# Row sums of reciprocals: loads of eight rows, the halves of every row added on TensorE, one product in four made on VectorE from a half copied to PSUM

## The chip, the cores and the metric

The kernel runs on one core of one Trainium2 chip. The metric is the device time of one execution in microseconds (us). Executions are compared with executions of the kernel before in the same rounds on the same chip.

## The reference

```python
def setup_inputs():
    batch, seq, dim = 32, 512, 1024
    return {"x": np.abs(np.random.randn(batch, seq, dim)).astype(np.float32) + 1e-6}

def reference(x):
    return np.sum(1.0 / x, axis=-1).astype(np.float32)
```

There are 16384 rows of 1024 float32, 128 rows in each of 128 partitions: 67.11 MB to read, 64 KB to write.

## The kernel before

Each row is split into two halves a and b of 512. As 1/a + 1/b = (a + b) / (ab), one reciprocal serves two elements: a product of the halves, then exp(-ln(ab)) on ScalarE, then a multiply by a + b with a running sum on VectorE. The sum a + b comes either from TensorE, as two matmuls with an identity that add up in PSUM (kind B), or is never formed: VectorE then multiplies the whole row of 1024 by the reciprocal, broadcast to both halves (kind A). Kind C gives one row whole to ScalarE.

```python
A, B, C = (2, 0, GP, False), (2, 0, GP, True), (1, 1, GP, False)
GROUPS = ([A, B, A, B, C, B, A, B] * 7 + ...)          # two rows in a group
xpool = ... bufs=16        # rpool, spool: 2 PSUM buffers each
for np_, ns, eng, on_pe in GROUPS:
    xt = xpool.tile([P, n, D], f32, tag="xt")
    nc.sync.dma_start(out=xt, in_=x_v[:, c0 : c0 + n, :])            # 1 MiB
    eng.tensor_tensor(out=pr, in0=xt[:, :np_, :H], in1=xt[:, :np_, H:], op=mult)
    if on_pe:
        for j in range(np_):
            for h in range(2):
                nc.tensor.matmul(sm[:, j, :], lhsT=ident,
                                 rhs=xt[:, j, h * H : (h + 1) * H],
                                 start=h == 0, stop=h == 1)
    ...                                                  # kind C's row on ScalarE
    nc.scalar.activation(out=pr, in_=pr, func=Ln, scale=S)
    nc.scalar.activation(out=rc, in_=pr, func=Exp, scale=-1.0)
    for j in range(np_):                  # rows of A: 1024 wide, of B: 512 wide
        nc.vector.tensor_tensor_reduce(out=row, in0=row, in1=rec, ..., accum_out=...)
```

## Time and profile before

| | before |
|---|---|
| time, median of the runs at hand before the change | 175.4 us |
| span of the profiled run | 172.6 us |
| rate of the loads in the middle (20 to 150 us) | 421 GB/s |
| rows that TensorE adds | 64 of 128 |
| TensorE busy, share of the span | 70% |

The prediction below shows the busy shares, the rates and the chain. Three groups of the same page give the durations that the argument uses; the columns are line, engine, operation, output and inputs, shapes, count, then busy us, mean ns of one, and idle time before them with what ended most of it.

```profile
L85 POOL TENSOR_TENSOR pr<-xt 128x1024 f32<-128x1024 f32 (+1 forms) x66 | 142.7, 2166 | 21.1 <-DMA xt<-in_x_dram 15.2
L90 PE MATMUL sm<-xt,ident 128*128 128x512 f32 x256 | 120.9, 617 | 47.0 <-DMA xt<-in_x_dram 45.0
L118 DVE CUSTOM_DVE_ANT_1 xt<-xt,rc 128x1024 f32<-128x1024 f32 x57 | 67.7, 1219 | 50.2 <-issue 27.2
```

GpSimd (POOL) has the least idle time, and TensorE's idle time is ended by landing loads: engines that wait for data. Each float32 matmul has two records in the trace. The mean of 617 ns is the length of one record; records overlap, and in a full stretch the next one starts 0.43 us later.

### The profile page before, as it was taken

How to read it: one execution, taken by the hardware profiler on the slowest of the kernel's cores; microseconds unless marked ns; L12 is line 12 of the kernel's file. 1: busy time of each engine (PE TensorE's matmuls, PEld its weight loads, DVE VectorE, ACT ScalarE, POOL GpSimd, SP SyncE). 2: the span in 40 equal slices, each digit the busy share in tenths (PEclk: the TensorE clock that was granted, in tenths of full speed). 3: DMA queues.
4: the chain of work that ended last, by engine and by line, in shares of the span. 5: the costliest groups of instructions: out<-in, count | busy, mean ns of one | idle time of the engine just before them, and what ended most of it. 6: DMA issues, size and time to landing. Idle time of an engine off the chain costs nothing.

```text
span 172.6 us, 1342 instructions
## 1 busy us (share of the span) xinstructions
PE 120.9 (70%) x256; PEld 47.4 (27%) x256; DVE 109.8 (64%) x243; ACT 142.0 (82%) x156; POOL 143.4 (83%) x72
## 2 busy tenths in 40 slices
PE   0099776767876767788666668977667876669480
PEld 0043322222332222233322223422222332223130
DVE  0009757874776757775578847468576755787791
ACT  2159989899878998889888996889988898988981
POOL 1599699969989799987999688997999979999920
PEclk9999999999999999999999996999999999999999
DMA  5999999999999999999999999999999999999500
GB/s 190 416 433 425 423 420 423 421 421 423 418 425 420 423 418 423 423 420 423 421 421 420 423 414 423 421 420 420 425 418 425 425 420 421 421 412 408 220 0 15
DMA packets 9799, 67.25 MB, mean 390 GB/s; under 512 B 1088, under 2 KB 1216, under 8 KB 1984
## 3 DMA queue, kind: packets, MB, share of 16 engines
q1 hardware_dynamic: 9792, 67.18, 94.0%
q8 instruction: 2, 0.03, 0.1%
q14 instruction: 5, 0.04, 0.1%
HBM read 67.11 MB, written 0.07 MB: 389 GB/s over the span
## 4 chain that ended last, share of the span: by engine, by line
DMA 78%; POOL 11%; ACT 2%; issue 2%; DVE 2%; SPq 1%; PE 1%; POOLq 0%; DVEq 0%
DMA xt<-in_x_dram 78%; POOL pr L85 11%; SPq L83 1%; ACT pr L106 1%; PE sm L90 1%; DVE xt L118 1%; ACT rc L111 1%; DVE pr L118 0%; ACT pr L111 0%; DVE pr L85 0%; POOLq L85 0%; DVE sums L118 0%; DVEq L118 0%; DVEq L157 0%
## 5 line engine op out<-in xcount | busy, mean ns | idle before, releaser
L85 POOL TENSOR_TENSOR pr<-xt 128x1024 f32<-128x1024 f32 (+1 forms) x66 | 142.7, 2166 | 21.1 <-DMA xt<-in_x_dram 15.2
L90 PE MATMUL sm<-xt,ident 128*128 128x512 f32 x256 | 120.9, 617 | 47.0 <-DMA xt<-in_x_dram 45.0
L118 DVE CUSTOM_DVE_ANT_1 xt<-xt,rc 128x1024 f32<-128x1024 f32 x57 | 67.7, 1219 | 50.2 <-issue 27.2
L106 ACT ACTIVATE pr<-pr 128x1024 f32<-128x1024 f32 (+1 forms) x67 | 65.0, 970 | 24.5 <-POOL pr L85 23.7
L90 PEld LDWEIGHTS sm<-xt,ident 128*128 128x128 f32 x256 | 47.4, 195 | 119.7 <-issue 57.8
L118 DVE CUSTOM_DVE_ANT_0 pr<-pr,sm 128x512 f32<-128x512 f32 x64 | 41.6, 685 | 9.8 <-ACT pr L111 8.6
L111 ACT ACTIVATE pr<-pr 128x1024 f32<-128x1024 f32 (+1 forms) x34 | 34.2, 1006 | 1.0
L111 ACT ACTIVATE rc<-pr 128x1024 f32<-128x1024 f32 (+1 forms) x33 | 29.9, 906 | 0.8
L118 DVE DVE_READ_ACCUMULATOR2_ANT sums<- 128x1 f32 x121 | 10.0, 82 | 0.0
L99 ACT ACTIVATE xt<-xt 128x1024 f32<-128x1024 f32 x7 | 7.3, 1041 | 0.0
L98 ACT ACTIVATE xt<-xt 128x1024 f32<-128x1024 f32 x7 | 7.3, 1040 | 0.0
L55 ACT ACT_TABLE_LOAD x1 | 1.3, 1283 | 0.7 <-PEq L146 0.7
L99 ACT ACTIVATION_READ_ACCUMULATOR xt<-xt 128x1 f32 x7 | 1.3, 186 | 0.0
L85 DVE TENSOR_TENSOR pr<-xt 128x512 f32<-128x512 f32 x1 | 0.7, 689 | 0.0
masks.py:197 POOL MEMSET ident<- 128x128 f32 x1 | 0.2, 204 | 0.3 <-POOLq L146 0.3
masks.py:199 POOL TENSOR_SCALAR_AFFINE_SELECT ident<-ident 128x128 f32<-128x128 f32 x1 | 0.3, 292 | 0.1
L146 POOL MEMSET const-float32-0.0<- 128x1 f32 x1 | 0.1, 98 | 0.2 <-issue 0.2
L146 POOL MEMSET const-bfloat16-1.0<- 128x1 bf16 x1 | 0.1, 101 | 0.0
L146 POOL MEMSET const-uint8-127<- 128x1 uint8 x1 | 0.1, 101 | 0.0
L146 POOL MEMSET const-float32-1.0<- 128x1 f32 x1 | 0.1, 98 | 0.0
## 6 DMA issues: line engine op xcount, KB each, us to landing
xt<-in_x_dram SPq DMA_DIRECT2D x61, 1024.0 KB, 19.8
xt<-in_x_dram SPq DMA_DIRECT2D x6, 512.0 KB, 15.6
out_dram<-sums SPq DMA_DIRECT2D x1, 64.0 KB, 1.5
```

Of the source, the lines that this page charges most:

```text
L55: nc.scalar.add_instruction(mybir.InstLoadActFuncSet(name=nc.get_next_instruction_name(), act_func_set_id=act_sets.index("natural_log_exp_ ...
L83: nc.sync.dma_start(out=xt, in_=x_v[:, c0 : c0 + n, :])
L85: eng.tensor_tensor(out=pr, in0=xt[:, :np_, :H], in1=xt[:, :np_, H:], op=mult)
L90: nc.tensor.matmul(sm[:, j, :], lhsT=ident, rhs=xt[:, j, h * H : (h + 1) * H], start=h == 0, stop=h == 1,)
L98: nc.scalar.activation(out=xt[:, j, :], in_=xt[:, j, :], func=Ln)
L99: nc.scalar.activation(out=xt[:, j, :], in_=xt[:, j, :], func=Exp, scale=-1.0, accum_out=sums[:, c0 + j : c0 + j + 1],)
L106: nc.scalar.activation(out=pr, in_=pr, func=Ln, scale=S)
L111: nc.scalar.activation(out=rc, in_=pr, func=Exp, scale=-1.0)
L118: nc.vector.tensor_tensor_reduce(out=row, in0=row, in1=rec, scale=S, scalar=0.0, op0=mult, op1=add, accum_out=sums[:, c0 + j : c0 + j + 1],)
L146: nc = _bacc.Bacc("TRN2", target_bir_lowering=False, num_devices=1)
```

## The change

The intent: larger transfers, which shrink row by row at the end so that little work is left after the last byte; a relief of VectorE from rows 1024 wide and of GpSimd from one product in four. VectorE makes that product from one half in SBUF and one in PSUM, to which TensorE copies it. A load holds one or two chunks. A chunk is the rows that are worked as one piece: one product on GpSimd for most of its rows, one Ln and one Exp on ScalarE for all of them.

```diff
+    LOADS = (
+        [[(4, 1), (4, 1)]] * 12
+        + [[(4, 1), (3, 1)], [(3, 1), (3, 1)], [(3, 1), (2, 1)], [(4, 1)]]
+        + [[(3, 1)], [(2, 0)], [(2, 1)], [(1, 0)], [(1, 1)], [(1, 1)]]
+    )
+    DIRECT = 126
-    xpool = ctx.enter_context(tc.tile_pool(name="xpool", bufs=16))
+    xpool = ctx.enter_context(tc.tile_pool(name="xpool", bufs=4))
...          spool: 6 PSUM banks for sums, bpool: 2 for copies
+        for m, v in chunks:                       # m rows, v products on VectorE
+            g = m - v
+            if g:
+                nc.gpsimd.tensor_tensor(
+                    out=pr[:, :g, :], in0=xc[:, :g, :H], in1=xc[:, :g, H:], op=mult
+                )
+            for j in range(g, m):
+                if c0 + q + j >= DIRECT:
+                    b = xc[:, j, H:]
+                else:
+                    b = bpool.tile([P, H], f32, tag="b")
+                    nc.tensor.matmul(b, lhsT=ident, rhs=xc[:, j, H:])
+                i = nc.vector.tensor_tensor(
+                    out=pr[:, j, :], in0=xc[:, j, :H], in1=b, op=mult
+                )
+                keep(i)                           # VectorE's order is fixed
+            if waiting:
+                sum_rows(*waiting)                # sums of the chunk before
+            for j in range(m):
+                s = spool.tile([P, H], f32, tag="s")
+                for h in range(2):
+                    nc.tensor.matmul(s, lhsT=ident, ...)
...          Ln, Exp on the whole chunk
```

More of the change, by code (lines that the diff above doesn't have):

```diff
@@ L33 @@
     S = float(2**17)
-    GP, DV = nc.gpsimd, nc.vector
-    A, B, C = (2, 0, GP, False), (2, 0, GP, True), (1, 1, GP, False)
-    GROUPS = (
-        [A, B, A, B, C, B, A, B] * 7
-        + [A, B, A, B, A]
-        + [(1, 0, GP, True), (1, 0, GP, False)] * 2
-        + [(1, 0, GP, True), (1, 0, DV, True)]
+    LOADS = (
+        [[(4, 1), (4, 1)]] * 12
+        + [[(4, 1), (3, 1)], [(3, 1), (3, 1)], [(3, 1), (2, 1)], [(4, 1)]]
+        + [[(3, 1)], [(2, 0)], [(2, 1)], [(1, 0)], [(1, 1)], [(1, 1)]]
     )
+    DIRECT = 126
     Ln = mybir.ActivationFunctionType.Ln
@@ L62 @@
     )
-    xpool = ctx.enter_context(tc.tile_pool(name="xpool", bufs=16))
+    xpool = ctx.enter_context(tc.tile_pool(name="xpool", bufs=4))
+    epool = ctx.enter_context(tc.tile_pool(name="epool", bufs=1))
     ppool = ctx.enter_context(tc.tile_pool(name="ppool", bufs=4))
     opool = ctx.enter_context(tc.tile_pool(name="opool", bufs=1))
-    rpool = ctx.enter_context(
-        tc.tile_pool(name="rpool", bufs=2, space=bass.MemoryType.PSUM)
-    )
-    spool = ctx.enter_context(
-        tc.tile_pool(name="spool", bufs=2, space=bass.MemoryType.PSUM)
+    spool = ctx.enter_context(
+        tc.tile_pool(name="spool", bufs=6, space=bass.MemoryType.PSUM)
+    )
+    bpool = ctx.enter_context(
+        tc.tile_pool(name="bpool", bufs=2, space=bass.MemoryType.PSUM)
     )
@@ L77, with sum_rows @@
     make_identity(nc, ident)
-    c0 = 0
-    for np_, ns, eng, on_pe in GROUPS:
-        n = np_ + ns
-        xt = xpool.tile([P, n, D], f32, tag="xt")
-        nc.sync.dma_start(out=xt, in_=x_v[:, c0 : c0 + n, :])
-        pr = ppool.tile([P, np_, H], f32, tag="pr")
-        eng.tensor_tensor(out=pr, in0=xt[:, :np_, :H], in1=xt[:, :np_, H:], op=mult)
-        if on_pe:
-            sm = spool.tile([P, np_, H], f32, tag="sm")
-            for j in range(np_):
-                for h in range(2):
-                    nc.tensor.matmul(
-                        sm[:, j, :],
-                        lhsT=ident,
-                        rhs=xt[:, j, h * H : (h + 1) * H],
-                        start=h == 0,
-                        stop=h == 1,
-                    )
-        for j in range(np_, n):
-            nc.scalar.activation(out=xt[:, j, :], in_=xt[:, j, :], func=Ln)
-            nc.scalar.activation(
-                out=xt[:, j, :],
-                in_=xt[:, j, :],
-                func=Exp,
-                scale=-1.0,
-                accum_out=sums[:, c0 + j : c0 + j + 1],
-            )
-        nc.scalar.activation(out=pr, in_=pr, func=Ln, scale=S)
-        if on_pe:
-            rc = pr
-        else:
-            rc = rpool.tile([P, np_, H], f32, tag="rc")
-        nc.scalar.activation(out=rc, in_=pr, func=Exp, scale=-1.0)
-        for j in range(np_):
-            if on_pe:
-                row, rec = rc[:, j, :], sm[:, j, :]
-            else:
-                row = xt[:, j, :].rearrange("p (h e) -> p h e", h=2)
-                rec = rc[:, j, :].unsqueeze(1).to_broadcast([P, 2, H])
-            nc.vector.tensor_tensor_reduce(
-                out=row,
-                in0=row,
-                in1=rec,
+    keep = tc.keep_in_program_order
+    def sum_rows(c, rc, sm):
+        for j, s in enumerate(sm):
+            i = nc.vector.tensor_tensor_reduce(
+                out=rc[:, j, :],
+                in0=rc[:, j, :],
+                in1=s,
                 scale=S,
@@ L125 @@
                 op1=add,
-                accum_out=sums[:, c0 + j : c0 + j + 1],
+                accum_out=sums[:, c + j : c + j + 1],
             )
+            keep(i)
+    waiting = None
+    c0 = 0
+    for k, chunks in enumerate(LOADS):
+        n = sum(m for m, _ in chunks)
+        if n > 3:
+            xt = xpool.tile([P, n, D], f32, tag="xt")
+        else:
+            xt = epool.tile([P, n, D], f32, tag=f"x{k}")
+        i = nc.sync.dma_start(out=xt, in_=x_v[:, c0 : c0 + n, :])
+        keep(i)
+        q = 0
+        for m, v in chunks:
+            xc = xt[:, q : q + m, :]
+            pr = ppool.tile([P, m, H], f32, tag="pr")
+            g = m - v
[6 more added lines that the diff above has]
+                    b = xc[:, j, H:]
+                else:
+                    b = bpool.tile([P, H], f32, tag="b")
[3 more added lines that the diff above has]
+                )
+                keep(i)
+            if waiting:
+                sum_rows(*waiting)
+            sm = []
+            for j in range(m):
+                s = spool.tile([P, H], f32, tag="s")
+                for h in range(2):
+                    nc.tensor.matmul(
+                        s,
+                        lhsT=ident,
+                        rhs=xc[:, j, h * H : (h + 1) * H],
+                        start=h == 0,
+                        stop=h == 1,
+                    )
+                sm.append(s)
+            nc.scalar.activation(out=pr, in_=pr, func=Ln, scale=S)
+            nc.scalar.activation(out=pr, in_=pr, func=Exp, scale=-1.0)
+            waiting = c0 + q, pr, sm
+            q += m
         c0 += n
     assert c0 == F, c0
+    sum_rows(*waiting)
     nc.sync.dma_start(out=out_v, in_=sums)
```

## The prediction

> **What bounds the kernel now.** I read the page first (busy shares, the slices, the chain of work that ended last), then the timeline of single engines, because busy shares alone do not say what an engine could do if it were kept full.
>
> From the page of the kernel before: busy time by engine, the granted clock and the rate of the transfers by slice, and the chain.
>
> ```profile
> span 172.6 us, 1342 instructions
> PE 120.9 (70%) x256; PEld 47.4 (27%) x256; DVE 109.8 (64%) x243; ACT 142.0 (82%) x156; POOL 143.4 (83%) x72
> ...
> PEclk9999999999999999999999996999999999999999
> ...
> GB/s 190 416 433 425 423 420 423 421 421 423 418 425 420 423 418 423 423 420 423 421 421 420 423 414 423 421 420 420 425 418 425 425 420 421 421 412 408 220 0 15
> ...
> DMA 78%; POOL 11%; ACT 2%; issue 2%; DVE 2%; SPq 1%; PE 1%; POOLq 0%; DVEq 0%
> ```
>
> The reader is to see a flat rate near 421 GB/s from the second slice almost to the end, and a chain that is 78% transfers. The input is 128 rows per partition, 67.11 MB; 67.11 / 421 = 159.4 us. About 3 us lie before the stream runs and about 10 after it, which gives the span of 172.6. So the input stream is the bound, and the only gain open to any change is in those two ends. Each four rows arrive in 4 x 0.524 = 2.1 MB / 421 GB/s = 4.98 us; every engine has to do four rows in less than that.
>
> Now what TensorE needs. The timeline of PE in the middle, and of the weight loads (PEld) in one of those bursts and at the start:
>
> ```profile
> 63.63 3.67 PE L90 MATMUL sm<-xt,ident 128*128 128x512 f32 x8 [1.36 <-DMA xt<-in_x_dram]
> 68.55 3.67 PE L90 MATMUL sm<-xt,ident 128*128 128x512 f32 x8 [1.24 <-DMA xt<-in_x_dram]
> 73.52 3.67 PE L90 MATMUL sm<-xt,ident 128*128 128x512 f32 x8 [1.30 <-DMA xt<-in_x_dram]
> ```
>
> ```profile
> 9.52 0.34 PEld L90 LDWEIGHTS sm<-xt,ident 128*128 128x128 f32 x1 [0.52 <-issue]
> 10.37 0.34 PEld L90 LDWEIGHTS sm<-xt,ident 128*128 128x128 f32 x1 [0.52 <-issue]
> ...
> 14.40 0.19 PEld L90 LDWEIGHTS sm<-xt,ident 128*128 128x128 f32 x1 [0.24 <-issue]
> 14.83 0.19 PEld L90 LDWEIGHTS sm<-xt,ident 128*128 128x128 f32 x1 [0.24 <-issue]
> 15.26 0.19 PEld L90 LDWEIGHTS sm<-xt,ident 128*128 128x128 f32 x1 [0.24 <-issue]
> 15.69 0.19 PEld L90 LDWEIGHTS sm<-xt,ident 128*128 128x128 f32 x1 [0.24 <-issue]
> 16.12 0.19 PEld L90 LDWEIGHTS sm<-xt,ident 128*128 128x128 f32 x1 [0.24 <-issue]
> 16.55 0.19 PEld L90 LDWEIGHTS sm<-xt,ident 128*128 128x128 f32 x1 [0.24 <-issue]
> ```
>
> The program has 128 matmuls (64 rows on TensorE, two halves each), the trace has 256: each float32 matmul runs as two records, each with its own weight load. In a full stretch the loads start 0.43 us apart ((16.55 - 14.40) / 5), so one float32 matmul of 512 columns costs 0.86 us, and one row (two halves) 1.72 us. A burst of 8 records is two rows: 8 x 0.43 = 3.44, plus the drain of the last, 3.67. One such burst comes per four rows arriving (4.97 us), and PE then waits 1.3 us for the next load. TensorE looks 70% busy with only half of the rows. That is the number that decides this case. At 9.5 to 12.1 the same loads stand 0.85 apart: the cold clock.
>
> The end, from the timeline of all engines: the last sum on VectorE, and the start of the store.
>
> ```profile
> 169.09 0.69 DVE L118 CUSTOM_DVE_ANT_0 pr<-pr,sm 128x512 f32<-128x512 f32 x1 [0.75 <-ACT pr L111]
> 169.70 0.08 DVE L118 DVE_READ_ACCUMULATOR2_ANT sums<- 128x1 f32 x1
> 169.81 0.35 SPq L131 DMA_DIRECT2D out_dram<-sums  x1
> ```
>
> From the end of the last sum (169.78) to the end of the span are 2.8 us.
>
> **What the Trainium skill says.** "TensorE: Matmul & The Clock Gate", section "Back-to-back issue gap", gives N / 2.4 + 2.5 ns for a warm stream: 216 ns for 512 columns of one pass. "FP8 and Floating Point Precision", section "TensorE Precision Notes", says that true FP32 takes four passes through the array: 4 x 216 = 863 ns. The trace agrees: 2 x 0.43 = 0.86 us. The first page's Part 1 on the clock gate says that the array starts at half clock for some 3.4 us of activity; the trace shows 0.85 against 0.43 us for about 4 us, and once more near 105 us after an idle stretch of 3 us. "DMA: Bandwidth & Descriptors", "Rules for kernel authors", asks for at least 1 MiB per transfer, and its Specifications give a fabric ceiling of 435 GB/s. The loads before are already 1 MiB, and 421 is 97% of that ceiling, so loads of eight rows have almost nothing left to win.
>
> **The change part by part.**
>
> Removed: the VectorE sums over 1024 columns with a broadcast reciprocal (57 of 1219 ns) and the seven rows that ScalarE did whole. Every row now goes by the halves: product of the halves, Ln, Exp of 512 columns, times the sum of the halves from TensorE.
>
> GpSimd: three rows of four. From 2365 ns for 1024 columns and 1273 for 512, 1536 columns cost 2365 + 1092 = 3.46 us per four rows, against 4.98 of arrival. It falls from 83% and stops being near the bound.
>
> ScalarE: 1055 ns for 1024 and 615 for 512 give about 1.94 us for 2048 columns, so Ln and Exp cost 3.9 us per four rows. Below 4.98.
>
> VectorE: one product at 0.69 and four sums, which start 0.61 apart in the trace before: 3.1 us per four rows.
>
> TensorE: four rows x two halves, plus one copied half = 9 float32 matmuls = 9 x 0.86 = 7.74 us per four rows. That is above 4.98, by 55%. TensorE becomes the bound, and the stream of loads waits for it through the four buffers of eight rows.
>
> Total: 128 x 2 = 256 matmuls for the sums. Of the 35 rows whose product VectorE makes, the last two are read directly, so 33 copies; the built program's order shows 33 too. 289 x 0.86 = 248.5 us of TensorE, in one unbroken run if nothing starves it.
>
> Start: PE needs the first load of eight rows. In the kernel before the first eight rows are loads 1 to 4: the first product starts at 5.58, the second load is there at 8.5, then 2.5 us each, so the fourth lands near 13.5. The order of bytes is the same, so PE starts near 13.5 instead of 8.5. The cold clock costs once about 2.3 us (five spacings of 0.85 instead of 0.43, and a partial one). The last matmul drains in 0.3, its sum takes 0.8 on VectorE (ScalarE's part of that row is ready, since the last loads landed long before), the store 2.8.
>
> Sum: 13.5 + 2.3 + 248.5 + 0.3 + 0.8 + 2.8 = 268.2 us of span. The measured run of the profile before was 174.8 for a span of 172.6, 2.2 more: 270.4, and I say 270.5 us.
>
> **The rivals.**
>
> First: the stream stays the bound, and the shorter tail wins some us (170 to 174). For it speaks that PE's busy share counts overlapping records and drains, so 70% overstates the need. Against it: the weight-load spacing is not a busy share, and within the bursts PE waited for no data. For this rival a float32 matmul would have to cost under 4.98 / 9 = 0.55 us, and the trace has none below 0.86.
>
> Second: a PSUM wait makes it worse than the TensorE sum. There are six banks for sums, four used per chunk, so the third row of a chunk waits for the first sum of the chunk before. Reckoned from the start of a chunk on PE: the copy is there at 0.9, the product at 1.7, Ln and Exp done at 5.7; VectorE, kept in order, first does the next chunk's product, possible at 7.74 + 0.9, so that the first sum ends near 10.2; PE asks for that bank at 7.74 + 0.86 + 2 x 1.72 = 12.0. About 1.8 us to spare, so no wait. If ScalarE or a semaphore took 2 us more than I reckon, a stall of 0.5 us in each of some 30 chunks would add 15 us: 285.
>
> Third: the clock. A TensorE that runs full could be granted less. Before, it was 0.99 on average with one dip to 0.6 after an idle stretch; a full engine has fewer such stretches, which speaks for none. A loss of 3% would add 8 us: 278.
>
> Fourth: the reverse, PE starts earlier or packs better than 0.43: at most the 5 us of the later start, 265.
>
> **Range and chances.** The central sum has one large term, measured in a stretch that is like the whole of the new kernel, and four small ones known to about 1 us each. The rivals add on the upper side, the fourth takes off a little: 264 to 278. For a time below 179 TensorE would have to do 9 matmuls in about 5.2 us per chunk; I see no way to it. Faster 0.01, same 0.01, slower 0.98.
>
> **What would show it.** PE has 578 records, loads of weights 0.43 us apart throughout, and the chain of what ended last is mostly PE instead of DMA. GB/s falls from 421 to about 2.1 MB / 7.74 us = 271 in the middle slices, after the first buffers are full; the queue's waits are for PE or its followers. PE's first matmul starts near 13.5 and the last one near 264. GpSimd, ScalarE and VectorE each fall to about half busy. Wrong would be: weight loads less than 0.4 apart; regular gaps in PE of over 0.3 us released by VectorE (the second rival); a granted clock below 0.97 in the middle slices (the third); GB/s still at 420 (the first).

## The result, and the profile after

Measured: 268.87 us (median of 4, 268.59 to 269.28) against 175.06 us before. The ratio is 1.536 (95% interval 1.531 to 1.542). Ratios here are the mean time of one kernel's fast runs over that of the other's of the same rounds, so not quite the ratio of the medians quoted.

The page of the changed kernel, as the prediction showed it of before:

```profile
span 267.5 us, 1796 instructions
PE 250.7 (94%) x578; PEld 110.7 (41%) x578; DVE 102.1 (38%) x291; ACT 125.6 (47%) x75; POOL 108.1 (40%) x41
...
PEclk9999999999999999999999999999999999999999
...
GB/s 289 431 436 431 431 431 446 417 439 201 432 88 392 157 353 277 225 402 78 441 108 382 245 246 308 107 364 20 374 0 265 423 404 9 0 0 0 1 0 10
...
PE 93%; DMA 5%; DVE 0%; ACT 0%; issue 0%; DVEq 0%
PE s L128 82%; PE b L117 11%; DMA xt<-in_x_dram 5%; DVE pr L81 0%; ACT pr L137 0%; ACT pr L136 0%; DVE pr L118 0%; DVEq L170 0%
...
L128 PE MATMUL s<-xt,ident 128*128 128x512 f32 x512 | 226.6, 595 | 0.0
```

TensorE is busy from its first matmul to its last: 250.7 us of 267.5, with no idle time at all before the sums. The chain, which was 78% transfers, is 93% TensorE: 82% sums, 11% copies. After the first slice the loads run near 431 GB/s for eight slices, until the four buffers are full, and then in bursts. The other three engines have fallen to 38 to 47%.

The timeline of TensorE at the start, then of VectorE at the end:

```profile
13.53 2.04 PE L117 MATMUL b<-xt,ident 128*128 128x512 f32 x2 [13.53 <-DMA xt<-in_x_dram]
15.37 8.49 PE L128 MATMUL s<-xt,ident 128*128 128x512 f32 x16
23.70 1.02 PE L117 MATMUL b<-xt,ident 128*128 128x512 f32 x2
24.55 7.03 PE L128 MATMUL s<-xt,ident 128*128 128x512 f32 x16
31.42 1.02 PE L117 MATMUL b<-xt,ident 128*128 128x512 f32 x2
```

```profile
264.32 0.69 DVE L81 CUSTOM_DVE_ANT_0 pr<-pr,s 128x512 f32<-128x512 f32 x1 [1.02 <-ACT pr L137]
264.94 0.08 DVE L81 DVE_READ_ACCUMULATOR2_ANT sums<- 128x1 f32 x1
```

A chunk of four rows takes 31.42 - 23.70 = 7.72 us, nine float32 matmuls of 0.858. The first chunk takes 10.2: its first five weight loads are 0.85 us apart, the cold clock. The profile puts the last sum's wait down to ScalarE; but TensorE's last matmul ends later by its record, at 264.20.

### The profile page after: what moved, and what is told of

Its sections match the earlier page's. It is cut to its first block, busy times and chain, and to the rows that moved or that the text cites. A ratio compares the mean times of both kernels' runs of the same rounds, so it can differ in the third digit from the quotient of the medians.

```text
span 267.5 us, 1796 instructions
## 1 busy us (share of the span) xinstructions
PE 250.7 (94%) x578; PEld 110.7 (41%) x578; DVE 102.1 (38%) x291; ACT 125.6 (47%) x75; POOL 108.1 (40%) x41
## 4 chain that ended last, share of the span: by engine, by line
PE 93%; DMA 5%; DVE 0%; ACT 0%; issue 0%; DVEq 0%
PE s L128 82%; PE b L117 11%; DMA xt<-in_x_dram 5%; DVE pr L81 0%; ACT pr L137 0%; ACT pr L136 0%; DVE pr L118 0%; DVEq L170 0%
## 5 line engine op out<-in xcount | busy, mean ns | idle before, releaser
L128 PE MATMUL s<-xt,ident 128*128 128x512 f32 x512 | 226.6, 595 | 0.0
L109 POOL TENSOR_TENSOR pr<-xt 128x1536 f32<-128x1536 f32 (+2 forms) x35 | 107.3, 3071 | 142.2 <-DVE sums L81 124.2
L128 PEld LDWEIGHTS s<-xt,ident 128*128 128x128 f32 x512 | 98.0, 191 | 123.9 <-issue 116.5
L136 ACT ACTIVATE pr<-pr 128x2048 f32<-128x2048 f32 (+3 forms) x37 | 62.2, 1681 | 135.9 <-DVE pr L118 117.9
L118 DVE TENSOR_TENSOR pr<-xt,b 128x512 f32<-128x512 f32 x33 | 22.7, 687 | 159.0 <-PE b L117 159.0
L81 DVE CUSTOM_DVE_ANT_0 pr<-pr,s 128x512 f32<-128x512 f32 x128 | 80.5, 681 | 4.0 <-issue 2.7
L137 ACT ACTIVATE pr<-pr 128x2048 f32<-128x2048 f32 (+3 forms) x37 | 62.2, 1680 | 1.2
L117 PE MATMUL b<-xt,ident 128*128 128x512 f32 x66 | 34.7, 608 | 13.5 <-DMA xt<-in_x_dram 13.5
L117 PEld LDWEIGHTS b<-xt,ident 128*128 128x128 f32 x66 | 12.7, 194 | 28.8 <-issue 28.8
L118 DVE TENSOR_TENSOR pr<-xt 128x512 f32<-128x512 f32 x2 | 1.4, 686 | 0.0
```

Source lines behind the costliest of these rows:

```text
L81: i = nc.vector.tensor_tensor_reduce(out=rc[:, j, :], in0=rc[:, j, :], in1=s, scale=S, scalar=0.0, op0=mult, op1=add, accum_out=sums[:, c ...
L109: nc.gpsimd.tensor_tensor(out=pr[:, :g, :], in0=xc[:, :g, :H], in1=xc[:, :g, H:], op=mult)
L117: nc.tensor.matmul(b, lhsT=ident, rhs=xc[:, j, H:])
L118: i = nc.vector.tensor_tensor(out=pr[:, j, :], in0=xc[:, j, :H], in1=b, op=mult)
L128: nc.tensor.matmul(s, lhsT=ident, rhs=xc[:, j, h * H : (h + 1) * H], start=h == 0, stop=h == 1,)
L137: nc.scalar.activation(out=pr, in_=pr, func=Exp, scale=-1.0)
```

## The experiments

Ten kernels ran, all correct by the comparison with the reference. That comparison is wide enough to pass the three whose sums are truncated.

### One term of the sum taken away: no copies (direct)

```diff
-    DIRECT = 126
+    DIRECT = 0
```

> VectorE reads both halves of every fourth row from SBUF, TensorE copies nothing: 256 float32 matmuls instead of 289. Theory (TensorE's matmul count sets the time): 33 x 0.858 us = 28.3 us less, 268.9 to 240.5 us, with PE still unbroken and a chunk of four rows taking 6.87 us. Rival (the wait of ScalarE for the copied half and VectorE's product, which fills most of VectorE's and ScalarE's idle time, is what spaces the chunks): the copies lie in the shadow of that chain and the time falls by more, since the chain loses the copy wait altogether; or by nothing, if VectorE and GpSimd both reading SBUF slow each other down (products above 0.75 us on VectorE).

Measured 240.94 us, ratio to before 1.379 (1.375 to 1.382). That is 27.9 us under the changed kernel for 33 matmuls, 0.85 us each: the time follows TensorE's count. From the page, the busy shares and the group of VectorE's products; then all of these products together, with the least, median and longest:

```profile
PE 221.9 (93%) x512; PEld 97.8 (41%) x512; DVE 119.5 (50%) x291; ACT 124.8 (52%) x75; POOL 116.5 (49%) x41
...
L118 DVE TENSOR_TENSOR pr<-xt 128x512 f32<-128x512 f32 x35 | 34.6, 990 | 13.3 <-DMA xt<-in_x_dram 13.3
...
L118 DVE TENSOR_TENSOR pr<-xt x35: 683/687/3914, 13.3 to 232.6; 128x512 f32<-128x512 f32 x35
```

The product on VectorE went from a mean of 687 to 990 ns, as the rival said, but it lies off the path: TensorE is busy without a break. The median says more than the mean: the product is not slowed a little each time. Four of the 35, all before 45 us, took 2.7 to 3.9 us, about the length of a GpSimd product (3.4 us), and began while one ran:

```profile
32.79 7.35 POOL L109 TENSOR_TENSOR pr<-xt 128x1536 f32<-128x1536 f32 x2 [2.95 <-DMA xt<-in_x_dram]
36.92 3.76 DVE L118 TENSOR_TENSOR pr<-xt 128x512 f32<-128x512 f32 x1
```

GpSimd ends at 40.14, and VectorE 0.54 us later. The Trainium skill, "SBUF — State Buffer", section "SBUF: two separate sides", says that a VectorE operation with two SBUF inputs and a GpSimd operation reading SBUF take an exclusive lock for a whole instruction, and the other fully blocks. These numbers agree. This is what the copy to PSUM buys, and here it costs 0.86 us of the bound engine each time.

### The start (split)

```diff
-        [[(4, 1), (4, 1)]] * 12
+        [[(4, 1)]] * 2
+        + [[(4, 1), (4, 1)]] * 11
```

> The first load of eight rows becomes two loads of four; all else as in the changed kernel. Theory (TensorE runs unbroken from its first matmul to the end, so its start counts in full): the first four rows land at about 8.5 instead of 13.5 us, the end comes 5.0 us earlier, 263.9 us. Rival (the start is hidden, something later sets the end): no change, within 1 us of 268.9. The cold stretch of TensorE, about 2.1 us, stays in both.

Measured 264.06 us, ratio 1.511 (1.507 to 1.514): 4.8 us less. TensorE's timeline shows the earlier start:

```profile
8.27 2.05 PE L118 MATMUL b<-xt,ident 128*128 128x512 f32 x2 [8.27 <-DMA xt<-in_x_dram]
```

5.26 us earlier at the start, 5.4 in the span. When an engine never stops, the wait for its first operand counts in full.

### The slack in PSUM (banks4, banks4k)

```diff
-        tc.tile_pool(name="spool", bufs=6, space=bass.MemoryType.PSUM)
+        tc.tile_pool(name="spool", bufs=4, space=bass.MemoryType.PSUM)
```

> Four PSUM banks for the sums instead of six. From the changed kernel's trace, after the copy of a chunk VectorE needs about 0.2 us to start the product, 0.6 for it and 0.6 for the first sum, and only then is the first bank free: TensorE, which would go on at once, should stall about 1.5 to 1.7 us in each of some 33 chunks of three or four rows: 50 to 56 us more, about 320 us, with idle time of TensorE put down to VectorE's sums. Rival (the six banks are not what keeps TensorE unbroken, its reordering or the later rows make up for it): under 5 us more.

Measured 273.81 us, ratio 1.566 (1.562 to 1.570): 5 us more instead of 50. This is the edge of what the rival had said, and the rival had named a cause of this kind: the scheduler reordered TensorE's work. With four banks it puts three copies in a row and then three chunks of sums, as the trace shows:

```profile
141.84 2.92 PE L117 MATMUL b<-xt,ident 128*128 128x512 f32 x6
```

So only about one chunk in three could wait, and the slack was not yet tested. The second try pins TensorE's order as well:

```diff
+                    i = nc.tensor.matmul(b, lhsT=ident, rhs=xc[:, j, H:])
+                    keep(i)
...                  the same for the matmuls of the sums
```

> Again four PSUM banks for the sums, but with TensorE's matmuls kept in the order of the changed kernel (with four banks alone the scheduler put three copies in a row ahead of three chunks of sums, so only one chunk in three could wait). Theory of the slack: in the changed kernel's trace the first sum of the chunk before is done about 1.55 us after TensorE has finished the copy, so with the bank of that sum needed at once TensorE idles about 1.5 us in each of the 25 to 33 chunks of four or three rows: 38 to 51 us more than the changed kernel, 307 to 320 us, idle time of PE put down to VectorE's sums. Rival (TensorE does not wait there for another reason): within 8 us of the 273.8 of the four banks without the order kept.

Measured 312.09 us, ratio 1.785 (1.780 to 1.790), 43 us more than the changed kernel. From TensorE's timeline:

```profile
145.57 1.02 PE L117 MATMUL b<-xt,ident 128*128 128x512 f32 x2
147.98 7.13 PE L129 MATMUL s<-xt,ident 128*128 128x512 f32 x16 [1.39 <-DVE sums L81]
```

After the copy TensorE stands idle until VectorE has finished the first sum of the chunk before; the trace lists 26 such waits. The next chunk's sums start 9.38 us after these (at 157.36), 1.66 more than the 7.72 of the changed kernel, and 26 x 1.66 = 43. The slack can be read from the same lines. Unhindered, the sums would start 0.858 after the copy, at 146.43; they start 1.55 later. Two banks more put that need off by two rows, 4 x 0.858 = 3.43 us, so the changed kernel has 3.43 - 1.55 = 1.9 us to spare. The prediction had reckoned 1.8.

### The same matmuls in one pass (onepass)

The sums read only the upper 16 bits of each float32, as bf16. The results are truncated; this is an experiment, not a version to use.

```diff
-                        lhsT=ident,
-                        rhs=xc[:, j, h * H : (h + 1) * H],
+                        lhsT=ident_b,
+                        rhs=xc.bitcast(bf16)[:, j, h * D + 1 : (h + 1) * D : 2],
```

> The sums of the halves are taken from the upper 16 bits of each float32 read as bf16, one record per matmul instead of two of double length; the copies stay float32. As many matmuls, loads, PSUM banks and VectorE instructions as in the changed kernel; the results are truncated (low by up to 0.8%, about 0.3% in the mean), on purpose. Theory (TensorE's four passes per float32 matmul are the bound): a one-pass matmul takes about 0.22 us, four rows 0.86 + 8 x 0.22 = 2.6 us, less than their arrival, and the stream of loads becomes the bound again at about 431 GB/s: 67.11 / 431 = 155.7 us, plus 3 before and 6 after, a span of 165, 166 to 169 us of time, below the kernel before. Rival (the order on VectorE, the buffers of eight rows or the PSUM banks hold the chunks apart): the time stays above 180 us.

Measured 174.36 us, ratio to before 1.000 (0.996 to 1.004). With as many matmuls, the same loads and banks, and VectorE's order kept (the scheduler put every second copy earlier among TensorE's sums), 94 us are gone. So what bound the changed kernel was the time of its float32 matmuls, not its buffers or VectorE's order. But 166 to 169 was expected, and the span of 172.2 is 7 us longer than the 165 reckoned. The stream ran at 429 GB/s from 20 to 150 us, but its end drags: 246 GB/s from 158 to 159, then 74, 41 and, from 161 to 162, 4. The expectation had its end at 3 + 155.7 = 158.7, so some 3 of the 7 us lie here. The rest lies behind the stream. ScalarE's timeline there:

```profile
152.44 1.91 ACT L139 ACTIVATE pr<-pr 128x2048 f32<-128x2048 f32 x1 [0.71 <-DVE pr L121]
154.39 1.91 ACT L140 ACTIVATE pr<-pr 128x2048 f32<-128x2048 f32 x1
156.21 1.47 ACT L139 ACTIVATE pr<-pr 128x1536 f32<-128x1536 f32 x1
```

The page names no bound here, as ScalarE is 72% busy; but at 152.4 it begins a chunk of four rows and has ten more rows to do, 14.7 us of Ln and Exp in all, while VectorE's queue adds waits. The expectation counted only the path of the last row behind the last byte, not the queue ahead of it. The sum ended at 169.7, some 8 us after the last bytes. TensorE is not ruled out in this tail: it fell back to the cold clock (0.88 granted over the run), waited 32.6 us for VectorE's sums, and one of its last copies took 1.91 us instead of 1.02.

### Is it ScalarE's queue? (onepass2, onepass3)

```diff
 onepass2, in place of the last eleven loads:
+        + [[(2, 1)] * 4, [(2, 1)] * 2, [(2, 1)] * 2, [(2, 1)] * 3]
+        + [[(2, 1)], [(2, 0)], [(2, 1)], [(1, 0)], [(1, 1)], [(1, 1)], [(1, 1)]]
```

> The one-pass sums again (truncated on purpose), with the last 32 rows worked in chunks of two instead of four and three, and four single rows at the end. Theory (the 7 us missed in the first one-pass run are ScalarE's queue: when its four-row chunk became ready at 152.4 it still had 14 rows or 14.8 us of Ln and Exp to do, while the stream ended near 157.5): chunks of two from row 96 on reach ScalarE about 5 us sooner after landing and it catches up while the stream still runs, so the last sum ends about 4 to 6 us after the last landing instead of 12: 167 to 170 us. Rival (PSUM banks, the copies behind them in TensorE's order, or a cold clock make the tail): 173 to 176 us as before.

Measured 178.17 us, ratio 1.019 (1.017 to 1.022): worse, not better, and outside both ranges. Smaller chunks inside loads of eight and six rows still wait for the whole load, and they cost ScalarE more per row: 2.1 us of work per two rows (1.04 + 1.06), and 16 rows took 17.14 us, 1.07 per row, against 3.82 / 4 = 0.96 in chunks of four and 1.22 of arrival. It could hardly catch up. GpSimd waited too: ten times, 13.4 us in all, for VectorE's sums, against once, 3.2 us, in onepass. The tile of products still has four buffers, and with chunks of two these hold eight rows. So this run doesn't test the queue alone.

```diff
 onepass3, one chunk per load, 8 buffers of four rows:
+        [[(4, 1)]] * 26
+        + [[(3, 1)]] * 3
+        + [[(2, 1)]] * 6
+        + [[(1, 0)], [(1, 1)], [(1, 1)]]
```

> The one-pass sums a third time (truncated on purpose), now with one load per chunk: 26 of four rows, three of three, six of two, three single. The second attempt failed because its chunks of two sat in loads of eight and six rows, and because ScalarE in chunks of two (1.06 us per row, and 0.16 more per row from waits) hardly gains on the arrival (1.22 us per row). ScalarE-queue theory, revised: a four-row chunk leaves ScalarE 7.3 us after its landing (3.46 GpSimd + 3.82 ScalarE); reckoned on through the threes, twos and ones, the last row leaves it about 4 us after the stream's end near 158.5, then 0.7 and 2.8: a span of 166, 167 to 172 us of time. Rival (whatever the chunks, VectorE's fixed order makes ScalarE wait for products queued behind sums, and the end stays some 12 us behind the stream): 174 us or more.

Measured 172.96 us, ratio 0.990 (0.988 to 0.992), between the two theories, a little above the range of the first. Of the loss, 1.4 us came back. ScalarE's timeline near the end shows a part of why not more:

```profile
151.75 1.06 ACT L140 ACTIVATE pr<-pr 128x1024 f32<-128x1024 f32 x1 [0.71 <-DVE pr L122]
...
165.86 0.63 ACT L140 ACTIVATE pr<-pr 128x512 f32<-128x512 f32 x1 [1.55 <-DVE pr L122]
```

ScalarE is now close behind the loads, but it waits five times, 3.7 us, for VectorE's products. In three of these waits (2.7 us, two of them shown) the product stands behind the sums of the chunk before in VectorE's fixed order. In the other two (0.9 us) VectorE itself waited 0.60 us for TensorE's copy. The last bytes move after 162 here too (12 GB/s from 162 to 163). So both theories hold a part of it. How the rest divides between queue, order and TensorE was not separated further.

### The larger loads alone (loads8)

```diff
 the kernel before, its groups taken from loads of 8 rows (14 of them), then 4, 4, 2 and six of 1
-    xpool = ctx.enter_context(tc.tile_pool(name="xpool", bufs=16))
+    xpool = ctx.enter_context(tc.tile_pool(name="xpool", bufs=4))
```

> The kernel before with only its loads changed: eight rows each for 112 rows, then 4, 4, 2 and single rows; its groups of two rows stay (the scheduler orders ScalarE a little otherwise). If larger loads are worth what the changed kernel's first slices show (431 instead of 421 GB/s), the stream ends about 4 us sooner; but GpSimd starts 8 us later (13.5 instead of 5.6) with 143 us of products and some 6 us of gaps, so it ends at 163 at the earliest, against 165 before. Expected 172 to 177 us, within 2% of before: the loads neither cause the slowdown nor give much. Rival (loads of eight rows in four buffers starve the engines): above 180 us.

Measured 178.92 us, ratio 1.024 (1.021 to 1.027), 2.4% slower, a little above what was expected. The stream is faster, 430 GB/s from 20 to 140 us, and ends sooner; but GpSimd starts at 13.4 and lags behind it. As its timeline shows, it then makes seven products in a row without waiting for a load, and the last three when the stream is over:

```profile
143.14 16.34 POOL L95 TENSOR_TENSOR pr<-big 128x1024 f32<-128x1024 f32 x7 [0.42 <-ACT rc L121]
...
164.92 3.75 POOL L95 TENSOR_TENSOR pr<-xt 128x512 f32<-128x512 f32 x3 [0.65 <-ACT rc L121]
```

Its last product ends at 168.7 (it was 165.1 before). ScalarE's order differs a little too, so the run doesn't show how much is GpSimd's. It shows that the loads of eight rows do not make the 94 us, and that alone they bring no gain.

### A correct version with TensorE under the rate of arrival (mixed, mixed2)

```diff
 loads of four rows, then 2 and 1; of each four rows TensorE adds two, VectorE does two whole
+    X, Y = (4, 0, 2), (4, 1, 2)      # rows, products on VectorE, rows TensorE does not add
+            rec = rc[:, j, :].unsqueeze(1).to_broadcast([P, 2, H])      # as before, in PSUM
```

> A correct kernel made from what the runs showed: loads of four rows, then two, then one; TensorE adds half of the rows only (138 float32 matmuls, 4 x 0.86 = 3.4 us per four rows), VectorE multiplies the other half whole against a reciprocal in PSUM, as in the kernel before; VectorE makes one product in eight rows direct from SBUF; chunks of four rows until row 96, then of two. Per four rows: GpSimd 4.0, ScalarE 4.0, VectorE 4.0, TensorE 3.4 us, all below the 4.87 of arrival at 431 GB/s. Theory (with TensorE below the arrival rate the stream is the bound, and a short queue at its end is what is left): 3 + 156 to 159 + 6 to 8, 167 to 172 us, 2 to 4% below the kernel before. Rival (VectorE reading both halves from SBUF beside GpSimd, and its order, hold the chunks up): 175 us or more.

Measured 177.86 us, ratio 1.017 (1.015 to 1.020). Two of its lines say what went wrong, the group of VectorE's products and a piece of the chain:

```profile
L111 DVE TENSOR_TENSOR pr<-xt 128x512 f32<-128x512 f32 x21 | 32.2, 1536 | 13.1 <-DMA xt<-in_x_dram 13.1
```

```profile
138.58 9.07 PE s L122 x20
```

The product direct from SBUF took 1.54 us beside a busier GpSimd (72% against 49%), and in the tail of two-row chunks the chain lay on TensorE again, 20 records at a stretch.

```diff
 mixed2: the half copied by TensorE again, one row in eight; 3, 2 and 1 rows at the end
+    LOADS = [X, Y] * 13 + [T, U, T] + [G, E] * 3 + [(1, 0, 1), (1, 1, 0), (1, 1, 0)]
+                nc.tensor.matmul(b, lhsT=ident, rhs=xt[:, g, H:])
```

> The correct mixed kernel again, mended where its trace showed the time to go: VectorE's products took 1.54 us with both halves from SBUF beside GpSimd, against 0.69 from a copy in PSUM, so the half is copied by TensorE again, but for one row in eight only (TensorE 8.5 float32 matmuls of 0.86 in eight rows... 4 x 2 + 1 = 9, 7.7 us of 9.74); and the tail, where TensorE ran unbroken for chunks of two rows from 138.6 to 157.2, now leaves more rows to VectorE and shrinks by threes, twos and ones. Theory (every engine under the arrival rate, short queue at the end): 168 to 172 us. Rival (VectorE at 80% with a fixed order keeps holding ScalarE's inputs back): 174 to 178 us, no faster than the kernel before.

Measured 175.84 us, ratio 1.006 (1.004 to 1.008). The products are back at 686 ns and all engines lie at 73 to 78%, yet ScalarE's last Exp ends at 170.8, against 169.1 in the kernel before. The rival's time was right; of its mechanism only a part is seen, six waits of ScalarE for VectorE's products, 5.1 us. What else sets this end stays open. No correct version here beats the kernel before.

## Why the prediction was right

Its one large term, float32 matmuls counted at the spacing of a full stretch, is the time. Step by step:

| step | predicted | measured |
|---|---|---|
| first matmul | 13.5 us | 13.53 us |
| records of TensorE | 578 | 578 |
| run of TensorE (2.3 + 248.5 + 0.3) | 251.1 us | 250.7 us, unbroken |
| GB/s once the buffers are full | 271 | 268 (60 to 160 us) |
| end of the last sum to the end of the span | 2.8 us | 2.5 us |
| span | 268.2 us | 267.5 us |
| time | 270.5 us | 268.87 us |

- TensorE as the bound: shown by direct (0.85 us per matmul removed) and by onepass (as many matmuls in one pass, 94 us less).
- The start in full: shown by split.
- The rival of the stream: it needed a float32 matmul under 0.55 us, and the trace has 0.858. Here the prediction misread a page: it took N / 2.4 + 2.5 ns as the spacing of a stream. The section "Back-to-back issue gap" gives this for a single matmul, and about 131 ns for a stream at 512 columns. Four times 131 is, as an estimate, 0.52 us, under the limit, so from that section alone the rival would have looked right. The measured spacing decides: 0.43 us between records of float32, and in onepass a pair of bf16 matmuls lasts 0.61 us where one lasts 0.387, so 0.22 apart. The prediction's 863 ns is an estimate from the single-matmul formula and the four passes; it fits, but what carries the prediction is the spacing that it read in the trace.
- The rival of the PSUM wait: rightly put aside, with 1.8 us of slack reckoned and 1.9 found by banks4k.
- The rival of the clock: the granted clock was 1.0, and a busy TensorE lost the cold stretch in mid-run, as expected; the one at its start stayed.
- What was too small, without effect: that loads of eight rows "have almost nothing left to win". They moved 430 to 433 GB/s against 421, 2 to 3% of the stream. Loads of four rows moved 427. Where the stream was the bound again, the engines behind it gave that back.
- The shares: VectorE came to 38%, GpSimd to 40, ScalarE to 47; "about half" was rough.

## What to carry to other kernels

Before giving an engine more of what it already does, take its spacing in a full stretch, multiply by the new count per unit of arriving data, and compare with the time in which that unit arrives: TensorE was 70% busy with half of the rows, and the other half could not fit. Weigh exchanges on the bound they create: adding one row's halves on TensorE cost 1.72 us of it, and saved VectorE some 0.5 us (1.219 to 0.685). And reckon the tail from the queue that the slowest stage still holds when the last bytes land, not only from the path of the last row; in onepass the end came 7 us after the one expected, which had reckoned neither with this queue nor with the dragging end of the stream.

## What the Trainium skill lacked or had wrong

- "DMA: Bandwidth & Descriptors", Specifications: the row of about 358 GB/s of HBM per core names no condition; the page says only further down that it is for both cores of a pair streaming. One core alone read 421 GB/s here for 130 us, and 433 with loads of 4 MiB.
- The same page, "Rules for kernel authors": at least 1 MiB per transfer for the most bandwidth. It does not say how much larger loads still bring when they are queued: 1 MiB gave 421, 2 MiB 427, 4 MiB 429 to 433 GB/s.
- "TensorE: Matmul & The Clock Gate", "LDWEIGHTS (loading the stationary operand)": P / 1.2, 107 ns for 128 columns. That is not so for float32: a load took 186 ns at the least, 190 in the median, and each float32 matmul had two of them; a bf16 load had a mean of 104 to 106 ns. The stream figure of the same page is compared with the trace under "Why the prediction was right". The page does not say that a float32 matmul is two records 0.43 us apart, which is what a reader meets in a trace.
